# A two-layer trunk kernel: opening products and loads in written order, other modulations later, h written straight from x

## The chip, the cores and the metric

The kernel runs on one core of a Trainium2 chip. The metric is the device time of one execution in microseconds (us). Before the change it is 1355.4 us, the median of 3 runs (1355.3 to 1356.14).

## What is computed

Two transformer layers work on 128 prompt tokens and 256 sample tokens (384 rows of 2048 numbers, float32). Each layer first makes a modulation from two condition vectors (one for the prompt, one for the samples), then normalises and modulates its input, and projects it:

```
m = silu(cond) @ w_mod + b_mod            # w_mod is 2048 x 6144
shift, scale, gate = split(m, 3)
h = rmsnorm(x, g) * (1 + scale) + shift   # 384 x 2048
u = h @ w_in                              # layer 0: 2048 x 7680; layer 1: 2048 x 5120
x = x + gate * (mixer(u) @ w_out)
```

The mixer of layer 0 is a gated linear recurrence beside attention with grouped heads, that of layer 1 windowed attention. Nothing of layer 0 after h can start before shift and scale are known, and these need 33.5 MB of w_mod.

## The kernel before, in words

Products of the projections run on TensorE (PE) in float32r, in three products each: a number is split in a high part, rounded by ScalarE (ACT), and the remainder, made by VectorE (DVE). For the weights these are `whi` and `wlo`, for the activations `hh` and `hl`; the products are hi·hi, hi·lo and lo·hi.

The opening of layer 0 works in five phases over k, the 16 blocks of 128 rows of the weights: blocks 0; 1 and 2; 3 to 5; 6 to 9; 10 to 15 (`START`, line 38). In each phase `start_products` runs six groups of 512 columns of w_in. A group has four accumulators `mm` (128x384 each); for each of its weight pieces (one or two blocks, 256 or 512 KB) `w_piece` loads `raw`, ACT casts it to `whi`, DVE makes `wlo`, and PE runs 12 products for a block, 24 for two. At the end of a group ACT copies (first phase) or DVE adds (later ones) the four accumulators into an SBUF tile. So there are 6, 6, 12, 12 and 18 weight pieces and 72, 144, 216, 288 and 432 products in the five phases.

While a phase's products run, `start_mod` (line 740) makes the shift and scale columns of the next phase: it loads w_mod in pieces `mraw` of 512 KB (8 pieces for two blocks, 4 for one), multiplies each with the padded condition columns `cs32` on PE into one bank `px`, copies the bank to `ev` (ACT), turns it with 128x128 transposes (PE), sums four rows of it (`ms`, DVE), and adds bias and gain (`modc`, `acol`, DVE). `modulate` (line 460) then scales x (tile tE for blocks 0 to 3, tF, tG, tH for the others) by the row of 1/rms `rb0` (DVE), applies scale and shift (ACT, in place), casts the result to `hh` (ACT) and makes `hl` (DVE). Only then can the products of that block start.

A second stream of work, the units (`mods`, line 776), makes the modulation of layer 1 and the gates of layer 0 on DVE: each unit loads 512 KB of w_mod (also a tile named mraw, line 271, in a ring of three) and adds it into `acc` with two instructions. `pump` (line 348) decides after each weight piece whether units are issued: it adds a rate to a budget (0.6 per piece in the opening, `RATE0`), and also asks that a running estimate of DVE's time stay below that of PE. All must be done near the end of layer 0's output projection.

All these loads go through the one queue of SyncE (SP), which issues in order; a load waits there for its buffer. The opening's w_mod pieces have a ring of four buffers (`RAWB`), its weight pieces a ring of three (`SRAW`). A scheduler in the framework decides the order of the instructions on each engine from dependences, priorities and its own estimate of time; the program's text decides only where these tie.

## Time and profile before

| | |
|---|---|
| runs, median (lowest to highest) | 1355.4 us (1355.3 to 1356.14) |
| profiled execution: time / span | 1356.77 us / 1355.0 us |
| mean granted clock of TensorE | 0.993 of full |
| PE, DVE, ACT, POOL busy | 97%, 75%, 48%, 5% of the span |
| read from HBM | 256 MB |

Times of a trace are microseconds from the start of the span. Waits of an instruction are put down to what released it last. An engine's busy time counts an instruction from its start to its modelled end, and matmuls overlap, so the distance from one start to the next tells more than the length of one.

### The profile page before, as it was taken

The numbers are of one execution on the slowest core, as the hardware profiler recorded it, in microseconds if no ns is written. First come the engines' busy times: TensorE is split into PE (matmuls) and PEld (weight loads), VectorE is DVE, ScalarE is ACT, GpSimd is POOL, SyncE is SP. The second block draws the span as 40 slices with busy tenths as digits, with TensorE's granted clock in tenths as the row PEclk, the third lists the DMA queues.
The fourth block names the chain that finished last, engine by engine and source line by source line (L and its number), as shares of the span: only waits on it lengthen the run. The fifth ranks groups of instructions, "written<-read, shape, count | busy, mean of one in ns | idle before, by whom it ended". The sixth has DMA issues, their size and how long they took to land.

```text
span 1355.0 us, 19101 instructions
## 1 busy us (share of the span) xinstructions
PE 1321.0 (97%) x7093; PEld 1125.7 (83%) x7093; DVE 1019.0 (75%) x1602; ACT 647.9 (48%) x1297; POOL 72.4 (5%) x84
## 2 busy tenths in 40 slices
PE   5899999999999999999999999999999999999998
PEld 4678888997888878787987887888888999998887
DVE  5678757998998745896998969995656664499743
ACT  4532233476655534755433347345766763352221
POOL 1000000000000021101000000200000101000000
PEclk8899999999999999999999999999999999999999
DMA  9989989755555334576778854784332345457642
GB/s 284 304 289 331 317 289 319 236 160 179 176 174 181 97 106 138 167 232 201 242 244 254 297 184 133 234 283 119 92 94 81 104 118 166 129 181 254 210 152 84
DMA packets 138317, 265.42 MB, mean 196 GB/s; under 512 B 8944, under 2 KB 46768, under 8 KB 138224
## 3 DMA queue, kind: packets, MB, share of 16 engines
q1 hardware_dynamic: 132592, 246.52, 56.9%
q0 software_dynamic: 5376, 17.60, 4.5%
q8 instruction: 56, 0.92, 0.3%
q14 instruction: 37, 0.30, 0.1%
q10 hardware_dynamic: 256, 0.08, 0.0%
HBM read 256.04 MB, written 8.13 MB: 195 GB/s over the span
## 4 chain that ended last, share of the span: by engine, by line
PE 91%; DMA 4%; DVE 3%; ACT 1%; POOL 1%; issue 0%; DVEq 0%; ACTq 0%; SPq 0%; POOLq 0%
PE mm L77 77%; PE px L77 14%; DMA raw<-in_l_w_in_dram 2%; DMA mraw<-in_l_w_mod_dram 1%; DVE wlo L77 1%; DVE acc L77 1%; DMA tB<-in_x_sample_dram 0%; ACT whi L370 0%; POOL sm L444 0%; DVE tB L77 0%; DMA rowc<-in_c_dram 0%; DVE tG L77 0%; ACT tE L469 0%; DVE tH L77 0%; POOL r L444 0%
## 5 line engine op out<-in xcount | busy, mean ns | idle before, releaser
L370 ACT CAST whi<-raw 128x1024 fp32r<-128x1024 f32 (+1 forms) x270 | 278.4, 1032 | 500.1 <-PE mm L77 393.7
L77 DVE TENSOR_TENSOR wlo<-raw,whi 128x1024 fp32r<-128x1024 f32 (+1 forms) x270 | 323.4, 1198 | 188.0 <-PE mm L77 148.6
L77 PE MATMUL mm<-whi,hh 128*128 128x512 f32 x1008 | 398.9, 396 | 0.0
L77 PE MATMUL mm<-wlo,hh 128*128 128x512 f32 x1008 | 391.7, 391 | 3.2 <-DVE wlo L77 3.2
L77 PE MATMUL mm<-whi,hl 128*128 128x512 f32 x1008 | 393.5, 391 | 0.6 <-DVE hl L77 0.6
L77 DVE SCALAR_TENSOR_TENSOR acc<-mraw,csil,acc 128x1024 f32<-128x1024 f32 x240 | 299.0, 1279 | 9.0 <-DMA mraw<-in_l_w_mod_dram 9.0
L77 PE MATMUL mm<-hh,whi 128*128 128x384 f32 x768 | 264.4, 347 | 7.1 <-ACT hh L471 4.6
L77 PE MATMUL mm<-hl,whi 128*128 128x384 f32 x768 | 259.2, 338 | 0.0
L77 PE MATMUL mm<-hh,wlo 128*128 128x384 f32 x768 | 254.5, 338 | 0.2 <-DVE wlo L77 0.2
L77 PEld LDWEIGHTS mm<-wlo,hh 128*128 128x128 f32 x1008 | 189.3, 188 | 42.7 <-DVE wlo L77 5.8
L77 PEld LDWEIGHTS mm<-whi,hl 128*128 128x128 f32 x1008 | 189.3, 188 | 40.8 <-DVE hl L77 1.5
L77 PEld LDWEIGHTS mm<-whi,hh 128*128 128x128 f32 x1008 | 189.4, 188 | 39.3 <-ACT tE L824 0.8
L77 PEld LDWEIGHTS mm<-hh,whi 128*128 128x128 f32 x768 | 145.3, 190 | 22.2 <-issue 10.1
L77 PEld LDWEIGHTS mm<-hh,wlo 128*128 128x128 f32 x768 | 144.8, 189 | 2.7 <-DVE wlo L77 1.0
L77 PEld LDWEIGHTS mm<-hl,whi 128*128 128x128 f32 x768 | 145.5, 190 | 1.2 <-issue 0.2
L623 ACT ACTIVATE p<-px,nb,rs 128x384 f32<-128x384 f32 (+1 forms) x72 | 42.4, 596 | 15.0 <-DVE nb L77 14.5
L77 PE MATMUL px<-mraw,cs 128*32 128x256 f32 (+1 forms) x576 | 40.4, 377 | 4.9 <-DMA mraw<-in_l_w_mod_dram 4.9
L633 ACT ACTIVATE p<-p,sum 128x384 f32<-128x384 f32 (+1 forms) x72 | 36.1, 540 | 15.1 <-DVE sum L77 13.2
L77 DVE TENSOR_REDUCE mx<-px 128x1 f32<-128x384 f32 (+1 forms) x54 | 29.7, 567 | 9.3 <-PE px L77 8.9
L77 PEld LDWEIGHTS px<-mraw,cs 128*32 128x32 f32 x576 | 16.3, 114 | 20.0 <-issue 8.2
L77 PEld LDWEIGHTS px<-ct,p 128*128 128x128 f32 x168 | 20.1, 141 | 8.3 <-issue 2.8
L444 POOL TENSOR_TENSOR rs<-rs,nhalf 128x12 f32<-128x12 f32 x6 | 14.7, 2450 | 227.5 <-DVE rs L77 227.5
(415 smaller groups left out, 1228.5 us busy)
## 6 DMA issues: line engine op xcount, KB each, us to landing
raw<-in_l_w_in_dram SPq DMA_DIRECT2D x194, 512.0 KB, 3.9
mraw<-in_l_w_mod_dram SPq DMA_DIRECT2D x192, 512.0 KB, 5.0
raw<-in_l_w_out_dram SPq DMA_DIRECT2D x64, 512.0 KB, 4.9
raw<-in_l_w_in_dram SPq DMA_DIRECT2D x12, 256.0 KB, 6.6
tK<-in_l_b_mod_dram POOLq DMA_DIRECT2D x6, 256.0 KB, 6.0
y1d<-tA POOLq DMA_DIRECT2D x2, 768.0 KB, 5.2
tD<-y1d POOLq DMA_DIRECT2D x2, 768.0 KB, 6.0
tL<-y1d POOLq DMA_DIRECT2D x2, 768.0 KB, 6.2
```

The source lines that it names most:

```text
L77: return f(*a, **k)
L370: nc.scalar.copy(hi, raw)
L444: nc.gpsimd.tensor_tensor(out=out, in0=out, in1=nhalf[:, 0:out.shape[1]], op=ALU.pow)
L623: nc.scalar.activation(p[:, j], ss[j], AF.Exp, bias=nb[:, j:j + 1], scale=rs[:, i + j:i + j + 1], accum_out=sm[:, j:j + 1])
L633: nc.scalar.activation(p[:, j], p[:, j], AF.Copy, scale=sm[:, j:j + 1])
```

## The change

Six edits, all in the opening of layer 0.

- **Order.** In the first two phases the products, w_mod products and transposes on PE, and the loads of weights and of w_mod on SP, keep the order of the program's text (`pin`).
- **Units.** The rate is a list by phase: none in the first two, 0.6 in the third and fourth, 1.0 in the fifth. A unit's load is issued behind the last weight load of the text. By program order, 7 units' loads stood in the first two phases before and none now; VectorE's accumulations (two per unit) stand at 14, 32 and 61 after the second, fourth and fifth phase before, at 0, 28 and 56 now; they are level at 96 some 50 weight pieces after the opening, and from there PE's order is almost the same to the end.
- **Idle tiles.** Six of the eight w_mod pieces for blocks 1 and 2 go to the tiles of hh and hl of later blocks, which are idle then, and not to the ring of four.
- **h from x.** For the first block of a phase ACT writes `hh` straight from x with scale and shift, and DVE computes the modulated x in place for `hl`; the other blocks go through x as before. The work goes block by block.
- **Scaling by rb0.** Instead of within `modulate`, each block's product with `rb0` stands at the start of its modulation; those of later blocks are ordered behind the first `hl`.
- **Pace.** The next phase's modulation is spread over one weight piece less (two in the first phase), with a step of its own between the copy to `ev` and the transposes.

```
-RATE0 = 0.6
+RATE0 = (0.0, 0.0, 0.6, 0.6, 1.0)
...
+    last_w = [None]
+    pinned = {"t": False, "s": False}
+    def pin(ins, queue):
+        if pinned[queue]:
+            tc.keep_in_program_order(ins)
+        return ins
...
-            nc.sync.dma_start(raws[kt], I[f"l{l}_w_mod"][kt * P:kt * P + P, c0:c0 + 1024])
+            with tc.issue_after(last_w[0].ins):
+                nc.sync.dma_start(raws[kt], I[f"l{l}_w_mod"][kt * P:kt * P + P, c0:c0 + 1024])
...
-        nc.sync.dma_start(raw, w_view(w, kt, nk, c0, n))
+        last_w[0] = pin(nc.sync.dma_start(raw, w_view(w, kt, nk, c0, n)), "s")
...
-    def modulate(l, q, xt, rb, hq=None, parts=((0, 4),)):
-
-        hh, hl = hq_tiles(q) if hq is None else hq
-        for k0, k1 in parts:
-            x = xt[:, k0:k1]
-            nc.vector.tensor_tensor(out=x, in0=x, in1=rb.unsqueeze(1).broadcast_to([P, k1 - k0, T]), op=ALU.mult)
-            for k in range(k0, k1):
-                for c, s in CT:
-                    kt = 4 * q + k
-                    nc.scalar.activation(xt[:, k, s], xt[:, k, s], AF.Identity, bias=modc[l][:, kt, c:c + 1],
-                                         scale=acol[l][:, kt, c:c + 1])
-            nc.scalar.copy(hh[:, k0:k1], x)
-            nc.vector.tensor_tensor(out=hl[:, k0:k1], in0=x, in1=hh[:, k0:k1].bitcast(F32), op=ALU.subtract)
-        return hh, hl
+    def modulate(k, first):
+        x, (hh, hl) = xT[k // 4][:, k % 4], [t[:, k % 4] for t in h0[k // 4]]
+        for c, s in CT:
+            m, a = modc[0][:, k, c:c + 1], acol[0][:, k, c:c + 1]
+            nc.scalar.activation(hh[:, s] if first else x[:, s], x[:, s], AF.Identity, bias=m, scale=a)
+            if first:
+                nc.vector.tensor_scalar(out=x[:, s], in0=x[:, s], scalar1=a, scalar2=m, op0=ALU.mult, op1=ALU.add)
+        if not first:
+            nc.scalar.copy(hh, x)
+        return nc.vector.tensor_tensor(out=hl, in0=x, in1=hh.bitcast(F32), op=ALU.subtract)
...
-    h0 = [hq_tiles(q) for q in range(4)]
+    h0 = [hq_tiles(0)]
+    done0 = []
+    idle = ["hh1", "hl1", "hh2", "hl2", "hh3", "hl3"]
...
-                    nc.tensor.matmul(ps[c][:, 0:T], lhsT=wh, rhs=hh[:, kq], start=(kt + k == k0), stop=False)
...
+                    pin(nc.tensor.matmul(ps[c][:, 0:T], lhsT=wh, rhs=hh[:, kq], start=(kt + k == k0), stop=False), "t")
...
+            for i in range(k, k + nk):
+                x = xT[i // 4][:, i % 4]
+                if k:
+                    with tc.issue_after(done0[0].ins):
+                        nc.vector.tensor_tensor(out=x, in0=x, in1=rb0, op=ALU.mult)
+                else:
+                    nc.vector.tensor_tensor(out=x, in0=x, in1=rb0, op=ALU.mult)
...
-                    raw = wpool.tile([P, k8, n], F32, tag="raw", bufs=RAWB, name=nm("mraw"))
-                    nc.sync.dma_start(raw, w_view(I["l0_w_mod"], k8 * i, k8, D * (1 - part) + k * P, n))
+                    if k == 1 and idle:
+                        raw = hpool.tile([P, 4 * T], F32, tag=idle.pop(0), name=nm("mraw"))[:, 0:1024]
+                        raw = raw.rearrange("p (k c) -> p k c", k=k8)
+                    else:
+                        raw = wpool.tile([P, k8, n], F32, tag="raw", bufs=RAWB, name=nm("mraw"))
+                    pin(nc.sync.dma_start(raw, w_view(I["l0_w_mod"], k8 * i, k8, D * (1 - part) + k * P, n)), "s")
...
-                        nc.tensor.matmul(ps[32 * (j % 4):32 * (j % 4) + 32, part * n:part * n + n],
-                                         lhsT=cs32[:, kt, :], rhs=raw[:, j], start=(kt < 4), stop=(kt >= KT - 4))
+                        pin(nc.tensor.matmul(ps[32 * (j % 4):32 * (j % 4) + 32, part * n:part * n + n],
+                                             lhsT=cs32[:, kt, :], rhs=raw[:, j], start=(kt < 4), stop=(kt >= KT - 4)), "t")
...
             nc.scalar.copy(ev[:, 0:2 * n], ps[:, 0:2 * n])
+            yield
             cp = px()
             for b in range(2 * nk):
-                nc.tensor.transpose(cp[:, b * P:b * P + P], ev[:, b * P:b * P + P], ident)
+                pin(nc.tensor.transpose(cp[:, b * P:b * P + P], ev[:, b * P:b * P + P], ident), "t")
...
-            modulate(0, k // 4, xT[k // 4], rb0, h0[k // 4], ((k % 4, k % 4 + nk),))
+            for i in range(k, k + nk):
+                if len(h0) <= i // 4:
+                    h0.append(hq_tiles(i // 4))
+                m = modulate(i, i == k0)
+                done0.append(m)
             yield
...
-    pace[1] = RATE0
+    pinned["t"] = pinned["s"] = True
...
+        pace[1] = RATE0[i]
         nxt, n_nxt = iter(()), 0
         if i + 1 < len(phases):
             k2, k3 = phases[i + 1]
-            nxt, n_nxt = start_mod(k2, k3), 4 * (k3 - k2)
-        n = len(first) * len(pairs(k0, k1))
+            nxt, n_nxt = start_mod(k2, k3), 4 * (k3 - k2) + len(pairs(k2, k3))
+        n = len(first) * len(pairs(k0, k1)) - (2 if i == 0 else 1)
         done = 0
         for j, _ in enumerate(start_products(k0, k1)):
-            while done < (j + 1) * n_nxt // n:
+            while done < min(n_nxt, (j + 1) * n_nxt // n):
                 next(nxt, None)
                 done += 1
             pump()
         for _ in nxt:
             pass
+        pinned["t"] = pinned["s"] = i < 1
         if i == 1:
             load_params()
```

On SP, at the start of the first phase's weights, before the change (raw: weights; line 748: w_mod of the opening; line 271: units; the tiles' numbers tell them apart):

```order
L368 DMA raw_328<-in_l_w_in_dram 128x512
L748 DMA mraw_347<-in_l_w_mod_dram 128x4x256
L368 DMA raw_361<-in_l_w_in_dram 128x512
L748 DMA mraw_379<-in_l_w_mod_dram 128x4x256
L368 DMA raw_393<-in_l_w_in_dram 128x512
L748 DMA mraw_411<-in_l_w_mod_dram 128x4x256
L748 DMA mraw_417<-in_l_w_mod_dram 128x4x256
L271 DMA mraw_424<-in_l_w_mod_dram 128x1024
L271 DMA mraw_426<-in_l_w_mod_dram 128x1024
L368 DMA raw_436<-in_l_w_in_dram 128x512
L748 DMA mraw_454<-in_l_w_mod_dram 128x4x256
L271 DMA mraw_460<-in_l_w_mod_dram 128x1024
```

And now, in the same place (line 379: weights, line 771: w_mod of the opening):

```order
L379 DMA raw_323<-in_l_w_in_dram 128x512
L771 DMA mraw_344<-in_l_w_mod_dram 128x4x256
L771 DMA mraw_350<-in_l_w_mod_dram 128x4x256
L379 DMA raw_364<-in_l_w_in_dram 128x512
L771 DMA mraw_382<-in_l_w_mod_dram 128x4x256
L771 DMA mraw_388<-in_l_w_mod_dram 128x4x256
L379 DMA raw_402<-in_l_w_in_dram 128x512
L771 DMA mraw_420<-in_l_w_mod_dram 128x4x256
L771 DMA mraw_426<-in_l_w_mod_dram 128x4x256
L379 DMA raw_440<-in_l_w_in_dram 128x512
L771 DMA mraw_458<-in_l_w_mod_dram 128x4x256
L771 DMA mraw_464<-in_l_w_mod_dram 128x4x256
```

Two w_mod pieces now stand between one weight piece and the next, and the three loads of units are gone from here.

On PE, at the end of the first phase, before (mm: products, the number tells the accumulator; px<-mraw: w_mod products, px<-ct,ev: the transposes; mm_503 is of the phase's last group, mm_561 of the next phase's first):

```order
L77 MATMUL mm_503<-hh_42_254,wlo_508 128x384
L77 MATMUL px_346<-mraw_522,cs_109 32x256 x4
L77 MATMUL px_346<-mraw_528,cs_109 32x256 x4
L77 MATMUL px_536<-ct,ev_534 128x128 x4
L77 MATMUL px_595<-mraw_596,cs_109 32x128 x8
L77 MATMUL px_595<-mraw_606,cs_109 32x128 x8
L77 MATMUL mm_561<-hh_42_254,whi_567 128x384
L77 MATMUL mm_562<-hh_42_254,whi_567 128x384
```

And now (mm_439 is of the fourth group of six, mm_495 of the fifth):

```order
L77 MATMUL mm_439<-hh_42_254,wlo_444 128x384
L77 MATMUL px_341<-mraw_458,cs_109 32x256 x4
L77 MATMUL px_341<-mraw_464,cs_109 32x256 x4
L77 MATMUL px_472<-ct,ev_470 128x128 x4
L77 MATMUL mm_495<-hh_42_254,whi_501 128x384
L77 MATMUL mm_495<-hl_43_255,whi_501 128x384
L77 MATMUL mm_495<-hh_42_254,wlo_503 128x384
L77 MATMUL mm_496<-hh_42_254,whi_501 128x384
```

The transposes that lead to blocks 1 and 2 stood behind all 72 products of the first phase, with only w_mod products between them and the products that need blocks 1 and 2; now the 24 products of the last two groups stand between.

On DVE, from the first scaling by rb0 (tE to tH: x of blocks 0 to 3, 4 to 7, and so on), before:

```order
L77 TENSOR_TENSOR tE_133<-tE_133,rb_238 128x384
L77 TENSOR_TENSOR tE_133<-tE_133,rb_238 128x768
L77 TENSOR_TENSOR tE_133<-tE_133,rb_238 128x384
L77 TENSOR_TENSOR tF_160<-tF_160,rb_238 128x768 x2
L77 TENSOR_TENSOR tG_187<-tG_187,rb_238 128x768
L77 TENSOR_REDUCE ms_314<-px_311 128x4
L77 TENSOR_TENSOR wlo_332<-raw_328,whi_330 128x512
L77 TENSOR_TENSOR modc_122<-ms_314,par 128x2 x2
L77 TENSOR_TENSOR tG_187<-tG_187,rb_238 128x768
L77 SCALAR_TENSOR_TENSOR acol_124<-modc_122,par 128x2
L77 TENSOR_TENSOR tH_217<-tH_217,rb_238 128x768
```

And now:

```order
L77 TENSOR_TENSOR tE_133<-tE_133,rb_238 128x384
L77 TENSOR_REDUCE ms_309<-px_306 128x4
L77 TENSOR_TENSOR wlo_327<-raw_323,whi_325 128x512
L77 TENSOR_TENSOR modc_122<-ms_309,par 128x2 x2
L77 SCALAR_TENSOR_TENSOR acol_124<-modc_122,par 128x2
L77 TENSOR_SCALAR tE_133<-tE_133,acol_124,modc_122 128x128
L77 TENSOR_SCALAR tE_133<-tE_133,acol_124,modc_122 128x256
L77 TENSOR_TENSOR hl_43_255<-tE_133,hh_42_254 128x384
L77 TENSOR_TENSOR tE_133<-tE_133,rb_238 128x384 x3
```

The sum `ms` and what follows it for block 0 stood among the scalings of all 16 blocks; now they and the first `hl` come right after the scaling of block 0.

## Rows read from the trace of the kernel before

**Rows 1.** The page, part 1: busy time, share, instructions of each engine

```profile
PE 1321.0 (97%) x7093; PEld 1125.7 (83%) x7093; DVE 1019.0 (75%) x1602; ACT 647.9 (48%) x1297; POOL 72.4 (5%) x84
```

**Rows 2.** Windows, all engines: busy us (instructions), TensorE clock, DMA share, GB/s

```profile
58.00:92.00 34.00, 33.76 (x238) 29.94 (x242) 26.23 (x42) 8.52 (x11) 0.60 (x1) 0.92 0.85 287
...
92.00:214.00 122.00, 120.15 (x872) 97.88 (x861) 84.13 (x131) 38.38 (x56) 0.00 (x0) 1.00 0.93 311
...
214.00:290.00 76.00, 75.21 (x433) 75.20 (x434) 71.82 (x79) 42.51 (x51) 1.43 (x2) 1.00 0.71 233
...
440.00:500.00 60.00, 60.00 (x341) 50.93 (x340) 35.15 (x79) 29.53 (x71) 9.77 (x10) 1.00 0.36 103
```

**Rows 3.** Windows of 2 us around the starts of two stages

```profile
46.00:48.00 2.00, 2.00 (x14) 1.14 (x13) 1.28 (x1) 1.33 (x4) 0.00 (x0) 1.00 1.04 304
...
60.00:62.00 2.00, 2.00 (x8) 2.00 (x8) 0.85 (x3) 0.74 (x1) 0.00 (x0) 0.50 1.09 355
```

**Rows 4.** Windows: a full and an idle stretch of the DMA engines

```profile
26.00:48.00 22.00, 17.98 (x110) 12.92 (x103) 14.01 (x20) 12.75 (x28) 0.00 (x0) 0.84 1.04 355
...
66.00:70.00 4.00, 4.00 (x51) 3.69 (x49) 3.40 (x6) 0.00 (x0) 0.00 (x0) 1.00 0.03 8
```

**Rows 5.** Timeline of PE, first phase: start, length, instruction, wait before it

```profile
23.95 0.44 PE L77 MATMUL px<-ct,ev 128*128 128x128 f32 x2 [0.55 <-ACT ev L756]
...
29.41 1.08 PE L77 MATMUL px<-mraw,cs 128*32 128x256 f32 x8 [2.81 <-DMA mraw<-in_l_w_mod_dram]
...
30.43 1.01 PE L77 MATMUL mm<-hh,whi 128*128 128x384 f32 x2
```

**Rows 6.** Timeline of DVE, the chain to the first product

```profile
25.28 0.17 DVE L77 TENSOR_REDUCE ms<-px 128x4 f32<-128x16 f32 x1
...
25.37 0.68 DVE L77 TENSOR_TENSOR wlo<-raw,whi 128x512 fp32r<-128x512 f32 x1
...
25.96 0.23 DVE L77 TENSOR_TENSOR modc<-ms,par 128x2 f32<-128x2 f32 x2
...
26.98 0.15 DVE L77 SCALAR_TENSOR_TENSOR acol<-modc,par 128x2 f32<-128x2 f32 x1
...
29.38 0.55 DVE L77 TENSOR_TENSOR hl<-tE,hh 128x384 fp32r<-128x384 f32 x1
```

**Rows 7.** Timeline of ACT, the same chain

```profile
27.16 0.99 ACT L469 ACTIVATE tE<-tE,modc,acol 128x128 f32<-128x128 f32 x2
```

**Rows 8.** Timeline of PE from the first phase into the second

```profile
44.02 0.45 PE L77 MATMUL mm<-hh,whi 128*128 128x384 f32 x1 [1.13 <-ACT whi L370]
...
49.95 1.07 PE L77 MATMUL px<-mraw,cs 128*32 128x256 f32 x16
...
57.97 1.65 PE L77 MATMUL mm<-hh,whi 128*128 128x384 f32 x4 [4.58 <-ACT hh L471]
...
60.05 0.52 PE L77 MATMUL mm<-hh,whi 128*128 128x384 f32 x1
...
60.38 0.52 PE L77 MATMUL mm<-hl,whi 128*128 128x384 f32 x1
```

**Rows 9.** Timeline of PE at the end of the second phase

```profile
91.38 1.07 PE L77 MATMUL px<-mraw,cs 128*32 128x256 f32 x16
...
92.38 0.44 PE L77 MATMUL mm<-hh,whi 128*128 128x384 f32 x1
...
93.18 0.63 PE L77 MATMUL px<-ct,ev 128*128 128x128 f32 x4
```

**Rows 10.** DMA issues, 0 to 60 us: form, count, KB each, median us to landing

```profile
mraw<-in_l_w_mod_dram SPq DMA_DIRECT2D x24, 512.0 KB, 7.7
```

**Rows 11.** DVE by form: busy us, mean ns of one, idle before

```profile
L77 DVE SCALAR_TENSOR_TENSOR acc<-mraw,csil,acc 128x1024 f32<-128x1024 f32 x240 | 299.0, 1279 | 9.0 <-DMA mraw<-in_l_w_mod_dram 9.0
```

**Rows 12.** Timeline of PE into the fifth phase

```profile
213.16 0.66 PE L77 MATMUL px<-ct,ev 128*128 128x128 f32 x4 [0.71 <-ACT ev L756]
...
214.79 0.44 PE L77 MATMUL mm<-hh,whi 128*128 128x384 f32 x1 [0.98 <-ACT whi L370]
```

More of the change, by code (lines that the diff above doesn't have):

```diff
@@ L729, in start_group @@
                     wh, wl = hi[:, k, c * P:c * P + P], lo[:, k, c * P:c * P + P]
[L730 to L732 removed]
+                    pin(nc.tensor.matmul(ps[c][:, 0:T], lhsT=wh, rhs=hh[:, kq], start=(kt + k == k0), stop=False), "t")
+                    pin(nc.tensor.matmul(ps[c][:, 0:T], lhsT=wh, rhs=hl[:, kq], start=False, stop=False), "t")
+                    pin(nc.tensor.matmul(ps[c][:, 0:T], lhsT=wl, rhs=hh[:, kq], start=False, stop=(kt + k == k1 - 1)), "t")
             yield
```

2 lines of the change are left out of this document (removed).

## The prediction

> **What bounds the kernel now.** I read the page's busy times first: PE is busy for 1321.0 of 1355.0 us [rows 1], so at most 34 us of open waiting can be won, and all work that PE does stays. Then the windows by stage. In the fifth phase (214 to 290) PE ends 433 products in 75.21 us, 0.174 us each [rows 2], without a wait: that is its pace at the full clock, and nothing in the opening is to be won there. The third and fourth phase (92 to 214) have 2 us of idle PE, at a DMA rate of 311 GB/s [rows 2] where a full stretch reaches 355 [rows 4]: bound by PE, with loads close behind. So what is left lies before 92 us. There the timelines show two holes. The first product starts at 30.43, although block 0's transposes ran at 23.95; between them PE took w_mod products of the next phase that waited 2.81 us for their load [rows 5], and DVE put its sums behind scalings of other blocks [rows 6]. From the first phase to the second PE waits 4.58 us for hh before 57.97 [rows 8], and then the granted clock stands at 0.50 [rows 3], the 1.2 GHz level: from 60.05 to 60.38 a product takes 0.33 us, not 0.174 [rows 8]. Last, the DMA engines idle from 66 to 70 us at 8 GB/s [rows 4], where by the program's order SP stands before a w_mod piece whose buffer, one of four, isn't free: the loads in front of 92 us are held by order and buffers, not by the DMA engines.
>
> **The first product.** The transposes at 23.95 stand in both kernels. Behind them DVE now has, with nothing between, the sum 0.17, one wlo 0.68, two modc 0.23 and acol 0.15 [rows 6]: 1.2 us, to 25.7 with small gaps. ACT then writes hh itself, two instructions in 0.99 us [rows 7], to 26.7; the cast behind them is gone. The second product needs hl: the in-place x on DVE, which no trace shows (between the 0.15 of a tiny instruction and the 0.55 of a subtraction over 384 columns [rows 6]; I take 0.3, since it is done in two parts), and hl's own 0.55 [rows 6]. Products flow from 27.6, 2.8 us earlier.
>
> **The first phase.** 72 products at 0.174 are 12.5 us. The first twelve fall behind a wait and are reckoned at 0.33: 1.8 more. Eight w_mod pieces go in four pairs; a pair takes 1.0 us from 91.38 to 92.38 [rows 9], and I add 0.25 for the turn to and from products: 5.0. The transposes now stand right behind the pair that they wait for, so PE waits for the copy ev (0.71) and runs them (0.6) [rows 12]: 1.3. ACT casts the fourth group's weights only behind the copies of the results before; for PE's wait I take another 0.7, as for ev. Together 21.3, to 48.9. The loads don't hold this: 14 pieces of the new order hold 5.2 MB up to the last w_mod piece, 14.8 us at 355 GB/s [rows 4], so 38 even if they start only at 23; PE asks for it at 43. Three loads of units that stood between them are gone, which matters little here for that reason.
>
> **Into the second phase.** The 24 products behind the transposes take 4.2 us and cover the chain to hh of block 1: DVE's sums without an accumulation of 1.28 [rows 11] among them, ACT's two instructions, hl. I leave 0.1: full pace at 49.0. Before, the stage starts at 57.97 and runs at half clock until about 62 [rows 3, 8], which is worth 2 us: full pace from 60.0. Gain here 11.0. If that cover is gone, the 4.58 us of [rows 8] come back, and the clock with them.
>
> **The second phase.** 144 products 25.1 us; six pairs of w_mod pieces 7.5; two copies with transposes, now in line, 2.6. Loads: SP keeps the text's order, so a weight piece waits behind w_mod pieces whose buffers are freed by products two steps back. A piece lands 7.7 us after its issue (median, [rows 10]), a step of PE takes 24 x 0.174 + 1.25 = 5.4. With one step of lead each of five steps would wait 2.3, 11.5 in all; with two it waits nothing. Four w_mod and three weight buffers give mostly two: I take 1.0. The end is 49.0 + 36.2 = 85.2. Before, the same work (20 w_mod pieces, their transposes, 144 products) is done at 93.18 + 0.6 less the four products that went ahead [rows 9], 93.1. The gain has shrunk to 7.9, mostly because the transposes now stop PE.
>
> **Third and fourth phase.** The next phase's h is ready one piece sooner, and the copy ev has a step to itself, so the waits of 0.71 and 0.98 at the start of the fifth phase [rows 12] go, and what is late next is nothing that the trace shows: 1.5 gained. Against it, units: 28 accumulations here instead of 18, so five loads more, 2.6 MB, 7.4 us at 355 GB/s if nothing were spare. Spare are 355 - 311 GB/s over 122 us, 5.4 MB [rows 2, 4]. The cost is between nothing and 7.4; I take 1.5, near the lower end, since the spare is twice the need, but not nothing, since part of it stands where SP waits for buffers. VectorE's ten accumulations of 1.28 [rows 11] find 38 us of idle time [rows 2], and so do the smaller scalings and the in-place x, a few us in all.
>
> **Behind the opening.** Five accumulations are owed after the fifth phase, up to 13 later, and all are paid 50 pieces after the opening: 16.6 us of VectorE, against 24.9 idle from 440 to 500 [rows 2], so at no cost; bounds -1 and +4 (a quarter of it in PE's way).
>
> **Sum.** -7.9 - 1.5 + 1.5 + 0 = -7.9 from 1356.8, the profiled execution (its span of 1355.0 and 1.8 around it): 1348.9. That execution is 1.4 over the median of the runs, so **1347.5** as a median. All at the good ends (no load waits, transposes hidden, no cost of units): some 15 less, 1340.5. Debt of loads in full and the gain at the fifth phase lost: 1354.5.
>
> **Rivals.**
> *The loads' debt.* The third and fourth phase turn load-bound, and what was won in front is given back there: up to 7.4. For it: the DMA share is 0.93 already [rows 2]. Against it: the spare above. 1353, from 1350.5 to 1355.
> *The queue in text order (slower).* In the second phase SP stands before a w_mod piece whose buffer isn't free while the weights behind it are wanted, as at 66 to 70 before [rows 4], now at every step. If no lead builds up, a step takes the landing, 7.7 [rows 10], and a wlo of 1.3 (twice the 0.68 of half the columns, [rows 6]), 9.0 against 5.4: 3.6 lost on each of five steps, 18 in place of the 1.0 above, so 9 slower than before: 1364.5; with half of that price no change. It decides from 1.8 us per step on, where the gain is gone. For it: one queue, in order, with waits for buffers. Against it: six idle tiles let the ring of four start the second phase empty.
> *The clock stays low.* The first phase now alternates products with waits. At half clock its 60 other products cost 0.15 more, 9 us, and nothing is left: 1355.5. Against it: a wait of 1.13 us before 44.02 [rows 8] left the clock at 1.00 [rows 3]; only after the 4.58 was it 0.50. I see no wait over 1.3 there.
> The Trainium skill, page "TensorE: Matmul & The Clock Gate", section "HAM oscillation — how this bites in real kernels", describes this: a wait for a load in each step lets the gate close, and every step starts cold. By that rule it would be this rival; the trace agrees with the rule for the long wait and shows no such thing for the short ones.
> *More.* The second phase has no load waits and the scheduler hides more: 1341.
>
> **How the numbers follow.** A run can tell 0.2% here, 2.7 us: faster is under 1352.7, slower over 1358.1. The forecast (gain 4 to 11) has 0.56, more 0.09, the debt 0.17, the clock 0.08, the queue 0.10. Faster: 0.56 + 0.09 + half of the debt 0.09 = 0.74. Slower: three quarters of the queue and a quarter of the clock, 0.10. The same: the rest, 0.16. The range 1340.5 to 1354.5 holds the forecast, most of more and of the debt and a little of the clock, 0.8. The forecast's own range is 1344 to 1351.5.
>
> **What would show it.** In the trace after: the first product near 27, the second behind hl at 27.6; the second phase's first product near 48.5 with the clock at 1.00 behind it, not 57.97 at 0.50; its last near 85; the fifth phase starting 8 us earlier than 214.79 without a wait for a cast before it; the rest of PE alike. I am wrong if PE waits for raw or whi at each step of 49 to 85 (queue), if PE's idle time and the DMA share of the third and fourth phase both rise (debt), if the clock is 0.50 through 30 to 45 (clock), or if PE waits for wlo between 300 and 540 (VectorE's debt).

## The result: 1.6% slower, and the profile after

The changed kernel takes 1378.8 us (median of 4 runs, 1374.8 to 1381.5) where the kernel before, run beside it, takes 1355.8: a ratio of 1.0164, 95% interval 1.0137 to 1.0192. The forecast was 1347.5. The profiled execution has 1379.4 us and a span of 1377.6, 22.6 more than before.

PE's work has not grown by much: first its line of the page (busy us, share of the span, instructions), then windows of the trace after (columns as in [rows 2]). They hold the first phase, the second, the third with the first half of the fourth, the second half of the fourth, and the fifth.

```profile
PE 1328.6 (96%) x7093; PEld 1130.3 (82%) x7093; DVE 1021.2 (74%) x1626; ACT 650.6 (47%) x1303; POOL 77.3 (6%) x84
```
```profile
24.00:52.00 28.00, 22.82 (x143) 17.02 (x144) 16.09 (x37) 18.02 (x38) 0.00 (x0) 0.86 0.89 274
52.00:91.00 39.00, 35.34 (x284) 30.41 (x283) 22.56 (x44) 11.84 (x18) 0.60 (x1) 0.97 0.77 260
91.00:177.00 86.00, 83.80 (x602) 68.12 (x600) 66.39 (x106) 23.71 (x36) 0.00 (x0) 1.00 0.91 306
177.00:226.00 49.00, 39.60 (x251) 32.32 (x252) 28.35 (x41) 15.67 (x23) 0.00 (x0) 0.93 0.85 294
226.00:300.00 74.00, 74.00 (x431) 72.87 (x430) 67.66 (x75) 33.94 (x38) 1.44 (x2) 1.00 0.66 212
```

The second half of the fourth phase stands out, not the first two phases: 9.4 of 49 us without work on PE, and part of the rest at half clock. The mean DMA share of 0.85 hides two things: the DMA engines ran dry (0.01) while SP stood, and were full again (0.99) while PE waited.

```profile
198.00:200.00 2.00, 2.00 (x27) 0.99 (x25) 0.96 (x1) 0.00 (x0) 0.00 (x0) 1.00 0.01 2
...
216.00:218.00 2.00, 0.00 (x0) 0.00 (x0) 0.56 (x1) 2.00 (x4) 0.00 (x0) 1.00 0.99 345
```

The sharpest view is one that counts. Every trace holds the same 5328 products of the projections in the same sequence of phases (72, 216, 432, 720 and 1152 at the phases' ends), so the start of the n-th one can be compared between kernels. In the table below "before" gives its start in us, each other row the difference to it; `r` is the ratio to the runs of before, with its interval. The differences belong to the profiled execution, whose time stands beside the median.

| kernel | median | r | profiled | 1 | 72 | 96 | 216 | 432 | 576 | 672 | 720 | 864 | 1352 | 5328 |
|---|---|---|---|---|---|---|---|---|---|---|---|---|---|---|
| before | 1355.8 | | 1356.8 | 30.4 | 49.7 | 64.7 | 91.1 | 142.1 | 177.2 | 200.0 | 211.1 | 239.7 | 336.9 | 1349.9 |
| after | 1378.8 | 1.0164 [1.0137, 1.0192] | 1379.4 | −3.9 | +1.9 | −7.7 | −1.3 | −1.2 | −1.5 | +4.1 | +12.9 | +10.9 | +19.4 | +22.6 |
| e1 | 1372.1 | 1.0116 [1.0091, 1.0141] | 1369.2 | −3.5 | +1.8 | −9.1 | −3.3 | −3.7 | −2.3 | −2.6 | −2.0 | +2.1 | +9.2 | +12.5 |
| e2 | 1371.5 | 1.0109 [1.0085, 1.0133] | 1380.4 | −4.6 | +1.3 | −8.4 | +0.6 | +2.6 | +1.9 | +8.3 | +18.4 | +16.5 | +16.6 | +23.5 |
| e3 | 1366.3 | 1.0079 [1.0053, 1.0105] | 1365.0 | −3.4 | +1.0 | −9.8 | −3.5 | −5.2 | −8.3 | −6.3 | −4.0 | +0.4 | +8.2 | +7.6 |
| e4 | 1376.8 | 1.0148 [1.0124, 1.0173] | 1378.6 | −4.1 | −0.6 | −9.7 | −8.8 | −7.2 | −8.2 | −2.6 | +11.6 | +9.7 | +17.3 | +21.3 |
| e5 | 1364.6 | 1.0064 [1.0045, 1.0083] | 1363.8 | −0.9 | −3.9 | −4.3 | −6.1 | −5.1 | −5.4 | −6.2 | −5.0 | −0.3 | +7.4 | +6.9 |
| e6 | 1366.7 | 1.0079 [1.0058, 1.0099] | 1370.0 | −4.0 | −0.5 | −9.5 | −8.3 | −9.8 | −11.2 | −5.7 | +8.1 | +6.2 | +13.7 | +13.3 |
| e7 | 1359.3 | 1.0019 [1.0008, 1.0030] | 1358.0 | −4.4 | −2.3 | −11.3 | −8.8 | −10.4 | −11.2 | −7.1 | +3.0 | +1.0 | +1.2 | +1.2 |
| e8 | 1367.9 | 1.0083 [1.0065, 1.0100] | 1365.9 | −3.8 | +1.0 | −9.9 | −6.4 | −7.3 | −9.8 | −6.2 | +3.8 | +1.9 | +9.1 | +8.9 |
| e9 | 1353.5 | 0.9974 [0.9960, 0.9988] | 1355.3 | −4.0 | −0.4 | −9.4 | −7.7 | −7.8 | −6.4 | −6.8 | −6.2 | −1.5 | −1.7 | −1.8 |
| e10 | 1358.2 | 1.0012 [0.9996, 1.0028] | 1356.7 | −4.9 | +0.1 | −10.8 | −4.3 | −6.9 | −6.9 | −7.7 | −7.4 | −0.1 | −0.3 | −0.4 |
| e11 | 1354.0 | 0.9981 [0.9968, 0.9994] | 1357.3 | −2.1 | +2.0 | −7.1 | −6.1 | −6.9 | −5.4 | −5.8 | −5.2 | +0.1 | −0.2 | +0.4 |
| e12 | 1355.0 | 0.9976 [0.9960, 0.9992] | 1352.7 | −3.3 | +3.6 | −5.4 | −2.7 | −5.3 | −4.0 | −3.9 | −3.4 | −5.0 | −5.3 | −4.2 |
| e13 | 1370.7 | 1.0101 [1.0084, 1.0119] | 1367.7 | −4.2 | +0.4 | −10.5 | −5.6 | −5.8 | −7.5 | −5.0 | +3.2 | +1.2 | +8.3 | +10.9 |
| e14 | 1358.9 | 1.0015 [1.0002, 1.0029] | 1358.4 | −4.5 | +0.4 | −8.7 | −7.5 | −8.8 | −10.0 | −6.2 | +4.1 | +2.1 | +1.9 | +1.6 |
| e15 | 1355.7 | 0.9992 [0.9982, 1.0002] | 1355.3 | −5.0 | −0.6 | −9.7 | −7.9 | −8.4 | −10.3 | −9.2 | −0.8 | −2.1 | −2.3 | −1.7 |
| e16 | 1352.9 | 0.9973 [0.9964, 0.9983] | 1351.6 | −4.4 | −2.3 | −11.4 | −10.5 | −12.6 | −13.0 | −12.1 | −11.5 | −5.2 | −5.4 | −5.4 |
| e17 | 1346.5 | 0.9930 [0.9916, 0.9943] | 1348.5 | −4.4 | +0.3 | −8.7 | −7.7 | −9.3 | −9.7 | −8.9 | −8.3 | −8.2 | −8.4 | −8.4 |
| e18 | 1363.8 | 1.0058 [1.0046, 1.0071] | 1363.8 | −4.0 | −0.5 | −9.5 | −5.2 | −6.4 | −6.6 | −4.4 | −4.8 | −5.1 | −7.0 | +6.9 |

The row "after" splits the 22.6 us: −1.5 up to the 576th product (of 7.7 won at the 96th), +5.6 to the 672nd, +6.8 over the seam into the fifth phase to the 864th, +8.5 to the 1352nd, +3.2 behind.

How firm is a column? By the program's order PE, ScalarE, VectorE and SP do the same work in the same order in e6, e7 and e14 up to the 1300th product, in the changed kernel and e2 likewise, and in e16 and e17 up to about the 720th. Their rows still differ by up to 2.8 us at the 216th product and 5.5 at the 720th. So a difference of that size between two single traces can be the execution alone; the medians are firmer.

**The first two phases.** The hole of 4.58 us before 57.97 [rows 8] is gone: the second phase's first product, the 73rd, starts at 51.94 without a wait. PE's waits from the first product to the end of the second phase, and that product (start, length, instruction, the wait in brackets):

```profile
26.57 0.45 PE L77 MATMUL mm<-hh,whi 128*128 128x384 f32 x1 [2.16 <-ACT hh L476]
27.61 0.69 PE L77 MATMUL mm<-hl,whi 128*128 128x384 f32 x1 [0.60 <-DVE hl L77]
44.66 0.66 PE L77 MATMUL px<-ct,ev 128*128 128x128 f32 x4 [0.71 <-ACT ev L779]
49.48 0.44 PE L77 MATMUL mm<-hh,whi 128*128 128x384 f32 x1 [1.53 <-ACT tK L747]
51.94 0.53 PE L77 MATMUL mm<-hh,whi 128*128 128x384 f32 x1
64.23 0.44 PE L77 MATMUL px<-ct,ev 128*128 128x128 f32 x2 [0.49 <-ACT ev L779]
71.52 0.44 PE L77 MATMUL mm<-hh,wlo 128*128 128x384 f32 x1 [0.64 <-DVE wlo L77]
78.24 0.44 PE L77 MATMUL mm<-hh,whi 128*128 128x384 f32 x1 [1.18 <-ACT whi L381]
79.50 0.44 PE L77 MATMUL mm<-hh,wlo 128*128 128x384 f32 x1 [0.64 <-DVE wlo L77]
85.29 0.66 PE L77 MATMUL px<-ct,ev 128*128 128x128 f32 x4 [0.71 <-ACT ev L779]
```

The first product comes at 26.57 as forecast. At 49.48 the last group of the first phase (its 64th product) waits for an accumulator that ScalarE's copies of the group before (tK) have not emptied yet. In ScalarE's order they stand behind the modulation of blocks 1 and 2:

```profile
47.20 0.98 ACT L476 ACTIVATE hh<-tE,modc,acol 128x128 fp32r<-128x128 f32 x2
...
48.96 0.46 ACT L747 COPY tK<-mm 128x384 f32<-128x384 f32 x1
```

SP meanwhile stands before buffers (its queue; a long entry is a wait inside the row). Of the two windows below, the first shows the half clock in which the second phase starts, the second that the DMA engines then run dry:

```profile
47.41 2.81 SPq L379 DMA_DIRECT2D raw<-in_l_w_in_dram  x1
...
57.97 5.76 SPq L771 DMA_DIRECT2D mraw<-in_l_w_mod_dram  x3
...
64.39 6.11 SPq L771 DMA_DIRECT2D mraw<-in_l_w_mod_dram  x3
```
```profile
52.00:54.00 2.00, 2.00 (x8) 2.00 (x7) 0.00 (x0) 1.42 (x2) 0.00 (x0) 0.50 0.99 315
54.00:60.00 6.00, 6.00 (x61) 5.55 (x60) 4.75 (x7) 1.06 (x1) 0.00 (x0) 0.98 0.12 33
```

**The fourth phase.** SP first, then PE. SP stands from 193.87 to 199.6 inside a pair of w_mod pieces; the weight piece behind them is issued only at 200.16, and PE waits for its cast at 207.15, then 3.92 us before 218.23, still in the fourth phase; the starts that follow are 0.32 us apart for a while, not 0.174. By the program's order three weight loads for the work behind the opening stand in SP's queue ahead of the weight that 218.23 waits for. It is issued at 209.86, lands at 216.4 in full DMA engines, and its cast on ScalarE (217.15, last fence) comes 0.8 later, behind the scalings of the next phase's blocks.

```profile
193.87 5.70 SPq L771 DMA_DIRECT2D mraw<-in_l_w_mod_dram  x2
199.62 0.50 SPq L282 DMA_DIRECT2D mraw<-in_l_w_mod_dram  x1
200.16 0.42 SPq L379 DMA_DIRECT2D raw<-in_l_w_in_dram  x1
...
209.86 0.47 SPq L379 DMA_DIRECT2D raw<-in_l_w_in_dram  x1
```
```profile
179.01 0.45 PE L77 MATMUL mm<-hh,whi 128*128 128x384 f32 x1 [2.04 <-ACT whi L381]
...
207.15 0.44 PE L77 MATMUL mm<-hh,whi 128*128 128x384 f32 x1 [1.78 <-ACT whi L381]
...
213.66 0.66 PE L77 MATMUL px<-ct,ev 128*128 128x128 f32 x4 [0.71 <-ACT ev L779]
218.23 0.69 PE L77 MATMUL mm<-hh,whi 128*128 128x384 f32 x1 [3.92 <-ACT whi L381]
```
```profile
214.97 1.37 ACT L476 ACTIVATE tH<-tH,modc,acol 128x128 f32<-128x128 f32 x3 [1.37 <-DVE acol L77]
...
217.15 1.03 ACT L381 CAST whi<-raw 128x1024 fp32r<-128x1024 f32 x1
```

**At 336 us.** A unit's modulation ends here (its sums at 333.49, its copy ev on ScalarE, its transposes). ScalarE is behind, because Exp (L895, L896) and Ln (L856, L857) of the next heads alternate and each turn loads a table. Behind the wait the clock is at 0.50 (the window below): the twelve products after the transposes start 0.43 us apart, before the wait 0.23, which is some 2.4 us more, so the wait of 5.74 makes most of the 8.5.

```profile
333.49 1.06 PE L77 MATMUL px<-acc,ct 128*32 128x512 f32 x8
335.75 0.40 PE L77 MATMUL mm<-whi,hl 128*128 128x512 f32 x1
341.89 0.90 PE L77 MATMUL px<-ct,ev 128*128 128x128 f32 x3 [5.74 <-ACT ev L311]
```
```profile
344.00:346.00 2.00, 2.00 (x6) 1.53 (x5) 1.15 (x1) 0.68 (x2) 0.00 (x0) 0.50 0.50 104
```
```profile
322.32 1.04 ACT L381 CAST whi<-raw 128x1024 fp32r<-128x1024 f32 x1
323.37 1.28 ACT L856 ACT_TABLE_LOAD   x1
324.67 0.71 ACT L856 ACTIVATE tE<-tB,ct,lb 128x384 f32<-128x384 f32 x1
325.39 1.28 ACT L895 ACT_TABLE_LOAD   x1
...
327.23 1.28 ACT L857 ACT_TABLE_LOAD   x1
...
329.16 1.28 ACT L896 ACT_TABLE_LOAD   x1
...
333.31 1.28 ACT L856 ACT_TABLE_LOAD   x1
...
341.25 0.58 ACT L311 COPY ev<-px 128x512 f32<-128x512 f32 x1
```

The whole run has 11 table loads, before 7.

**Behind.** VectorE's waits for the units' loads (us in all, times, the longest) after, before, and in e3:

```profile
DVE acc L77 <- DMA mraw<-in_l_w_mod_dram: 34.8, 19, 5.3
```
```profile
DVE acc L77 <- DMA mraw<-in_l_w_mod_dram: 9.0, 7, 4.1
```
```profile
DVE acc L77 <- DMA mraw<-in_l_w_mod_dram: 7.1, 4, 3.6
```

### The profile page after: what moved, and what is told of

Read it like the earlier page. It is cut to its first block, busy times and chain, and to the rows that moved or that the text cites. A ratio compares the mean times of both kernels' runs of the same rounds, so it can differ in the third digit from the quotient of the medians.

```text
span 1377.6 us, 19123 instructions
## 1 busy us (share of the span) xinstructions
PE 1328.6 (96%) x7093; PEld 1130.3 (82%) x7093; DVE 1021.2 (74%) x1626; ACT 650.6 (47%) x1303; POOL 77.3 (6%) x84
## 4 chain that ended last, share of the span: by engine, by line
PE 84%; DVE 5%; DMA 5%; ACT 3%; issue 1%; POOL 1%; SPq 0%; ACTq 0%; DVEq 0%; POOLq 0%
PE mm L77 71%; PE px L77 14%; DMA raw<-in_l_w_in_dram 2%; DVE acc L77 2%; DMA mraw<-in_l_w_mod_dram 1%; DVE wlo L77 1%; ACT whi L381 1%; DVE tB L77 0%; DMA tC<-in_x_sample_dram 0%; POOL rs L455 0%; DMA rowa<-in_l_norm_dram 0%; DMA tab<-in_l_b_knorm_dram 0%; DVE tG L77 0%; DVE tH L77 0%; ACT junk L567 0%
## 5 line engine op out<-in xcount | busy, mean ns | idle before, releaser
L77 PE MATMUL mm<-hh,whi 128*128 128x384 f32 x768 | 266.8, 347 | 14.2 <-ACT whi L381 10.5
L77 PEld LDWEIGHTS mm<-hh,whi 128*128 128x128 f32 x768 | 146.0, 190 | 28.8 <-ACT whi L381 14.8
L641 ACT ACTIVATE p<-p,sum 128x384 f32<-128x384 f32 (+1 forms) x72 | 35.4, 540 | 13.2 <-DVE sum L77 11.3
L455 POOL TENSOR_TENSOR rs<-rs,nhalf 128x12 f32<-128x12 f32 x6 | 21.7, 3612 | 221.3 <-DVE rs L77 221.3
```

Of the source, the lines that this page charges most:

```text
L77: return f(*a, **k)
L455: nc.gpsimd.tensor_tensor(out=out, in0=out, in1=nhalf[:, 0:out.shape[1]], op=ALU.pow)
L641: nc.scalar.activation(p[:, j], p[:, j], AF.Copy, scale=sm[:, j:j + 1])
```

## The experiments

The theory after the first look: separate costs, one for each place above, and the dealing alone behind the fourth phase. The rivals were two of the forecast's: the debt of the units' loads, and the queue in text order.

**e1, the old dealing.** Where `n_nxt` turns of the next phase's modulation are dealt over `n` weight pieces of a phase; in the fourth phase the changed kernel deals 27 turns over 11 pieces, here it is 24 over 12 as before:

```
-nxt, n_nxt = start_mod(k2, k3), 4 * (k3 - k2) + len(pairs(k2, k3))
+gap = i < 2    # start_mod yields behind ev only with gap
+nxt, n_nxt = start_mod(k2, k3, gap), 4 * (k3 - k2) + (len(pairs(k2, k3)) if gap else 0)
...
-n = len(first) * len(pairs(k0, k1)) - (2 if i == 0 else 1)
+n = len(first) * len(pairs(k0, k1)) - (2 if i == 0 else 1 if i == 1 else 0)
```

> The changed kernel, but from the third phase on the w_mod pieces are dealt out as before: two per group of products in the fourth phase (24 pieces over 12 groups, no extra turn behind the copy ev), not 27 turns over 11. Theory (pacing): the 14 us that the changed kernel loses between the 432nd and the 720th product (PE waits 8.0 us for whi there, because three w_mod pieces in a row stand before a weight piece) go; the 720th product comes near 212 instead of 224, and the time is near 1366 (1363 to 1370) against 1378.8. Rival (debt of the units' loads): the 28 units' loads are still there and the fourth phase still loses over 8 us; 1374 or more.

The 720th product is 2.0 ahead: 1.7 lost since the 432nd where 14.1 were. The time gained only 6.7 and misses: 4.1 of the 14 only moved behind the 720th, and ScalarE's order changed along with it, to 13 table loads; to the 1352nd 7.1 were lost in another way (PE waits 4.3 for wlo at 310 to 345).

**e2, ev on VectorE.** `nc.scalar.copy(ev, ps)` in mod_part becomes `nc.vector.tensor_copy(ev, ps)`.

> The changed kernel, but the copy ev of a later modulation (mod_part) is made by VectorE instead of ScalarE. Theory (ScalarE's order): PE's wait of 5.74 us before 341.89 and the clock at half speed behind it come from ScalarE, whose Exp and Ln now alternate with a table load of 1.28 us each time; with the copy on VectorE, which is idle at 335 to 337, the 1352nd product stands about 11 later than before instead of 19.4, and the time is near 1370.5 (1368 to 1374). Rival (the sums themselves are late, or VectorE is as late as ScalarE): the wait stays over 3 us and the time over 1375.

From the 864th to the 1352nd 0.1 are lost instead of 8.5, and the median falls by 7.2, to the theory's time. (The profiled execution is 9 above the median; its 720th product is 5.5 later than in the changed kernel with the same order of work up to there.) ScalarE's loads fell to 9 as well, so the copy's new place and the order are not told apart; that the wait was ScalarE's is shown.

**e3, units' loads free.** `with tc.issue_after(last_w[0].ins):` taken away in mod_acc.

> The changed kernel, but the loads of the later modulations may be moved ahead of weight loads again, as before (no issue_after). Theory (late loads): VectorE's waits for mraw fall from 34.8 us towards the 9.0 of before, and the 4.6 us that the changed kernel loses behind 940 us go; the opening is touched by less than that: near 1374 (1371 to 1377). Rival (the loads go into the first two phases instead, ahead of their weights): the second phase gets longer by 4 us or more, and the time is 1379 or over.

Waits for mraw fall to 7.1, and nothing is lost behind the 1352nd any more, as expected; but the time misses: the gain is 12.5, since from the 432nd to the 720th only 1.2 are lost too. The theory had no reason for that. The edit also moved other loads: by the program's order SP's queue differs from the changed kernel's from the second phase on.

**e4, no text order.** `pinned` stays False.

> The changed kernel, but products and loads of the first two phases are not kept in the text's order. Theory (text order wins in the first phase and gives it back in the second): the 96th product stands at 60 or later instead of 57.0, the 216th within 3 us of 89.8, and the time is within 4 us of 1378.8. Rival (the queue in text order, which the prediction named as the slower case, is the cause): the 216th product comes before 86 and the time is under 1372.

The theory's time, but not its opening: without the order the 96th product is 9.7 ahead and the 216th still 8.8. So the order gives nothing in front and costs 7.5 by the 216th product, in the direction of the forecast's rival; the fourth phase then lost 18.8 and hid it.

**e5, the units' shift alone**, on the kernel before: `RATE0 = (0.0, 0.0, 0.6, 0.6, 1.0)`, `pace[1] = RATE0[i]` in the loop.

> The kernel before with one thing of the change: the later modulations get no turn in the first two phases (the list of rates 0, 0, 0.6, 0.6, 1.0); their loads may still be moved ahead of weights. Theory (the shift of these units by itself changes ScalarE's order): ScalarE gets 13 table loads where it had 7, and PE loses 4 to 9 us between the 1152nd and the 1352nd product as in the changed kernel; the opening is at most 3 us shorter: near 1360 (1356 to 1365) against 1356. Rival (the shift costs nothing, and relieves the first two phases of nine loads of 0.5 MB): 1352 or less.

The opening gains 6.1 at the 216th, more than thought; 4.8 go between the 432nd and the 864th, 7.7 from there to the 1352nd. ScalarE has 13 table loads. Moving the units is enough to bring a cost of that size in this stretch, though PE's waits fall otherwise: 3.75 for wlo before 322.28, where VectorE had stood 5.23 for ScalarE's Exp, and 2.24 for ev before 332.59.

**e6 to e8, combinations**: e6 is e3 and e4 together, e7 adds e2, e8 is e3 with only PE's products pinned, not the loads.

> The changed kernel without both orders: products and loads of the first two phases not kept in the text's order, and the units' loads free to go ahead of weights. Theory (the two costs add): the opening as without text order (the 216th product near 8.8 ahead of before, against 3.5 ahead with free loads alone), the fourth phase as with free loads (0 to 1 lost), the loss of 7.8 at the 1352nd product stays: near 1360 (1356 to 1363). Rival (free units' loads take the place of weights in the unpinned opening): the 216th product within 4 us of before and the time 1364 or more.

> As the run before (neither order), with the copy ev of a later modulation on VectorE. Theory (three separate causes): the wait of 5.8 for ev at the 1352nd product goes too, and about 8 us with it: near 1351 (1348 to 1355), faster than before. Rival (the ev's place in ScalarE's order stands for a delay that returns elsewhere): 1356 or more.

> The changed kernel with the units' loads free, and of the first two phases only PE's products kept in the text's order, not SP's loads. It tells which of the two orders costs the 6.3 us between the 96th and the 216th product. Theory (the queue of loads in text order, which stands before w_mod pieces whose buffers are not free): the loss falls to 2 us or less, 216th product 7 or more ahead of before, near 1362 against 1366. Rival (PE in text order, where transposes and products wait in line for ev, hh and wlo): the loss stays over 4 us and the time within 2 of 1366.

e6 misses: the opening adds up (−9.8 at the 432nd), but the fourth phase loses 17.9 with free loads, so e3's good one was not due to free loads alone. In e7 the cost at 336 us is gone (0.2 for 7.5), and the time misses by as much as the fourth phase. e8 divides the cost of the order at the 216th product: 3.5 ahead with both queues pinned, 6.4 with PE alone, 8.3 with none: 2.9 of SP, 1.9 of PE. Executions of the same order differ by up to 2.8 there, so the division is not shown; and its time, 1367.9, is no better than e3's and e6's.

**e9 to e12, all three undone**: e9 has e1, e2, e3 and e4, and in hgrn_prep holds each Ln behind the last Exp written before it (`with tc.issue_after(lexp[0].ins):`). e10 puts the text order back, e11 takes the idle tiles away (`idle = []`), e12 gives the units 0.6 in all phases.

> The changed kernel without either order (text order of the first two phases, units' loads behind weights), with two w_mod pieces per group from the third phase on as before, the ev of later modulations on VectorE, and the Ln of the next heads' preparation held behind the last Exp written before it, so that ScalarE changes tables less often. Left of the change: h straight from x, weights in idle tiles of h, units from the third phase on. Theory (the costs add): 11 us ahead at the 576th product as in the run before, still 8 to 10 ahead at the 720th, 4 lost at the seam to the fifth phase, nothing at the 1352nd: near 1350.5 (1347 to 1354). Rival (what is won in the opening meets the next bound, the loads of the fourth phase, whatever the pacing): 1355 or more.

> As the run before, but with products and loads of the first two phases in the text's order, as in the changed kernel. It prices that order with the other costs gone. Theory (the order costs at the second phase's steps what it costs with free loads): the 216th product 3.5 ahead of before where it is 8.8 without, and 5 to 7 us more than the run before: near 1356.5 (1353 to 1360). Rival (the order costs nothing, since what it loses in the second phase comes back in the third and fourth): within 2 us of the run before.

> As the first of these four runs, but the second phase's w_mod pieces go into the ring of four and not into idle tiles of h. Theory (the idle tiles let loads of the second phase start early): the 96th product comes 2 to 4 us later and the time is 1352.5 to 1354.5. Rival (without text order SP brings those loads early enough into the ring): within 1.5 us of the first run.

> As the first of these four runs, but the later modulations take their turns from the first phase on, at 0.6 per piece as before. Theory (the units' loads of the first two phases cost the opening what their removal gained alone, 4 to 6 us at the 216th product): 216th product 3 to 5 ahead of before, the fourth phase 1 to 2 shorter, near 1354 (1351 to 1357). Rival (the shift wins nothing in the end, since the loads come back in the third and fourth phase): 1351 or less.

e9 is faster than before, 0.9974, and its time is in the theory's range, but it is 6.4 ahead at the 576th product, not 11, and 4.7 went between the 720th and the 864th. The order's price is 4.7 us (e10 to e9, medians), a little under the theory; for the idle tiles the medians show nothing clear of noise (0.4; 2.3 at the 96th product, gone by the end: the rival). e12 is 5 less ahead at the 216th than e9, and in time not to be told from it; it is 3.4 ahead of e9 at the 864th: it loses nothing at that seam.

**e13 to e16, the dealing**: e13 is the changed kernel with a fifth w_mod buffer from the third phase on; e14 is e9 with the new dealing, e15 with only the `- 1`, e16 with only the turn behind ev.

```
+elif turn[0] % 5 == 4:
+    raw = spool.tile([P, k8, n], F32, tag="xw", bufs=1, name=nm("mraw"))
...
+turn[0] += k > 2
```

> The changed kernel with a fifth buffer for w_mod pieces from the third phase on (one more tile takes every fifth piece). Theory (SP stands before a w_mod piece whose buffer, one of four, is not free, while the weight piece behind it is wanted): the 14.1 us lost between the 432nd and the 720th product fall to 6 or less, and the time to 1366 to 1372. Rival (the fourth phase is short of load bandwidth, or of ScalarE): the loss stays at 11 or more and the time at 1375 or more.

> The version with all three undone, with the changed kernel's dealing of w_mod pieces in the third and fourth phase put back (a turn of its own behind ev, and all turns one group sooner: 27 over 11). Theory (this dealing is what costs the fourth phase): 10 to 15 us lost between the 432nd and the 720th product where that version lost 1.6, and a time of 1361 to 1368 against 1353.6. Rival (it needs the units' loads bound behind the weights, or another order besides): loss under 4, time under 1357.

> As the version with all three undone, but the w_mod pieces are dealt out one group sooner, without a turn of their own for ev (24 turns over 11 groups in the fourth phase). Theory (three w_mod pieces in a row are what hurts, and 24 over 11 has that in two groups, 27 over 11 in five): about 2/5 of the loss of the full dealing, 4 to 7 us between the 432nd and the 720th product. Rival (the last group without w_mod pieces is no loss at all): under 3.

> As the version with all three undone, but the copy ev of the opening's modulations has a turn of its own (27 turns over 12 groups in the fourth phase). Theory (three in a row in three groups of twelve, one of the three turns often empty): 2 to 5 us lost between the 432nd and the 720th product. Rival (it is the turn of ev that moves the pieces against the ring of four): 8 or more.

From the 432nd to the 720th product e14 loses 12.9, as its theory says, e15 7.6 and e13 9.0, both over theirs, e16 1.1, under it; e14's time is under its theory, e13's within. The columns between show why: two things were taken for one.

*The dealing.* From the 432nd to the 672nd product the six traces with the changed kernel's dealing and one order of SP's queue (after, e2, e4, e6, e7, e14) lose 2.7 to 5.8. All nine with turns over 12 pieces (e1, e5, e9 to e12, e16 to e18) lie between 1.1 gained and 2.0 lost, e13 with its fifth buffer loses 0.8, and e15 gains 0.8. By the program's order the dealing puts three w_mod pieces in a row four times: two of them are behind PE before the 576th product, where nothing is lost yet, and the loss comes behind it (after 5.6, e14 3.8 from the 576th). A row of three does not decide alone: in e3 and e8 the same dealing stands in another order of the queue, with such rows too, and they gain 1.1 and lose 1.1. In the medians the dealing costs 5.4 (e14 to e9), and the turn behind ev alone nothing (e16 to e9).

*The seam.* From the 672nd to the 864th, over the seam into the fifth phase, nearly all lose, whatever the dealing: after 6.8, e14 8.3, e15 7.1, e16 6.9, e13 6.3, e9 5.3, e1 4.7, e3 6.7, e5 5.9, the rest up to there 5.9 to 12.3; only e12 loses nothing. The dealing sets on which side of the 720th that falls.

**e17 and e18, the seam into the fifth phase.** In SP's order two to four weight loads for the work behind the opening stand ahead of the fifth phase's first weight, with the new dealing ahead of the fourth phase's last one too; in before there are two, in e12 none. e17 is e16 with an edge against that (w5 is the third weight load of the fifth phase); e18 adds rates of 0, 0.6, 0.6, 0.6, 0.6.

```
+with tc.issue_after(w5[0].ins) if tag == "raw" else nullcontext():
     last_w[0] = pin(nc.sync.dma_start(raw, w_view(w, kt, nk, c0, n)), "s")
```

> The best version so far (a turn for ev, the rest as all three undone), but the first weights of the work behind the opening may not be loaded ahead of the fifth phase's first three weight pieces. Theory (at the seam into the fifth phase the wanted weight stands behind two to four loads for later: PE waits 3.1 us for whi, then runs at half clock): 11.5 us ahead at the 720th product, still 10 or more ahead at the 864th instead of 5.2; near 1348 (1345.5 to 1351) against 1352.9. Rival (the later loads, now later themselves, are missed at the end of the fifth phase, or the loss at the seam is the units' debt of loads): 5 to 7 ahead at the 1352nd product, 1351.5 to 1355.

> As the run before, with the units' turns from the second phase on at 0.6 each, so that none are owed. Theory (the units' loads in the second phase cost PE there, and are nothing gained later once the seam is in order): 2 to 4 us less ahead at the 432nd product, near 1351 (1348 to 1354). Rival (what the shift wins in the opening is debt in the fourth and fifth phase in any case): within 1 us of the run before or faster.

e17 takes 1346.5 us, 0.9930 of before: the fastest of all, and the theory's time. From the 672nd to the 864th it loses 0.7, e16 6.9. At the 720th it is 8.3 ahead, not 11.5, though its order of work up to there is e16's: that part is the execution. At the seam in e16 (SP, ScalarE, PE) two later weights and a unit's load go first; the wanted weight is issued at 197.73 and lands 6.5 us later, its cast can start only at 204.29 (the view puts that wait down to DVE, but the load is what came last), and PE waits for that. Behind it two windows of e17: the last part of the fourth phase up to the seam, with the DMA engines full, and the fifth phase.

```profile
191.06 0.37 SPq L379 DMA_DIRECT2D raw<-in_l_w_in_dram  x1
195.62 0.37 SPq L379 DMA_DIRECT2D raw<-in_l_w_in_dram  x1
196.04 1.63 SPq L282 DMA_DIRECT2D mraw<-in_l_w_mod_dram  x1
197.73 0.43 SPq L379 DMA_DIRECT2D raw<-in_l_w_in_dram  x1
```
```profile
204.29 1.04 ACT L381 CAST whi<-raw 128x1024 fp32r<-128x1024 f32 x1 [2.68 <-DVE acc L77]
```
```profile
205.39 0.69 PE L77 MATMUL mm<-hh,whi 128*128 128x384 f32 x1 [3.07 <-ACT whi L381]
```
```profile
169.00:203.00 34.00, 33.45 (x228) 26.96 (x226) 23.43 (x31) 9.59 (x13) 0.00 (x0) 1.00 1.01 346
203.00:282.00 79.00, 79.00 (x467) 76.60 (x467) 73.60 (x87) 37.47 (x43) 1.44 (x2) 1.00 0.70 231
```

e18 was badly dealt: its rates sum to 28.8 units by the end of the opening, not 32.4 as in before and e17, so units were owed after all. They fall due near 716 us, and PE waits for VectorE's last sums, through ScalarE's cast:

```profile
716.09 0.79 PE L77 MATMUL px<-ahi,ones_r 128*128 128x512 f32 x1 [9.62 <-ACT ahi L337]
```

Its time misses. Up to the 1352nd product e18 is 7.0 ahead, so its question is half answered: nothing is lost at the seam, with more of the units moved or with fewer.

## Why the prediction was wrong, step by step

- **First product near 27, the next at 27.6.** Right: 26.57 and 27.61.
- **First phase, 21.3 us.** Too short by some 3: the 72nd product is 1.9 later than before. The wait of 1.53 for the copies tK (49.48) was in no term, the products behind it run at half clock, 0.32 apart, and so does the first pair of w_mod pieces, 1.9 us at 31.43 and not 1.0.
- **Into the second phase, full pace at 49.0.** Wrong. The chain to hh is covered, as said, and the 73rd product waits for nothing; but it starts at 51.94, and the clock is 0.50 at 52 to 54, which was to have gone. The cover had a price that was not counted: with hh moved forward in ScalarE's order the copies of the first phase's results stand behind it.
- **Second phase, load waits 1.0.** Undersized: PE waits 2.5 for weights there (71.52, 78.24, 79.50). The text order costs 3.4 (e10 to e9) to 7.5 us (after to e4) by the 216th product, so the slower rival "queue in text order" had the direction, at less than its price; how much of it is SP's, and how much PE standing in line for ev and tK, is open. By the forecast's own count the work done at 93.1 before is done at 90.0, 3 us sooner and not 7.9.
- **Third and fourth phase, −1.5 + 1.5 = 0.** This step failed most: 12.1 us from the 432nd product to the 864th. The extra turn was counted as a gain (the wait for ev; 0.71 of it is still there at 213.66) and the pace as nothing. What the forecast left out is the order in SP's queue. 27 turns over 11 weight pieces put three w_mod pieces in a row before SP's ring of four where two were; SP falls behind, and the weights come late: 2.7 to 5.8 lost by the 672nd product with this order of the queue, at most 2.0 with the turns over 12 pieces, 0.8 with a fifth buffer. And the loads for later work go ahead of the wanted weights at the seam: 6.8 here, 5 to 12 in the others with such loads ahead, 0.7 with the order mended (e17). The rival "debt" named the right stage, but not the cause: with the five more units' loads still there e17 loses 1.1 in all of it. Bandwidth is still part of the price: the DMA engines are full at the seam (1.01 in e17's window at 346 GB/s), so each load of 512 KB put ahead takes some 1.5 us from the wanted one, an estimate from that window.
- **Behind the opening, 0 (−1 to +4).** The 3.2 behind the 1352nd product are inside the bounds, by another way: not VectorE's debt, but units' loads that `issue_after` binds behind weights through the whole kernel. In the kernels without that edge nothing is lost there (−0.6 to +1.1), e18's late units apart. The 8.5 around 336 us were in no term: with the units moved, ScalarE's order changes tables where one of them ends.
- **Range and rivals.** 1378.8 lies beyond all of them, since each took one mechanism alone and the costs came together. The rival of the clock did not come as stated (1.00 from 34 to 50 us), but the argument against it, no wait over 1.3, did not hold: behind waits of 1.53 (before 49.48) and 2.04 (before 179.01) the granted clock stood at 0.50 at 52 to 54 and 0.53 at 182 to 184. Two slips in the working change little: the clock rival's 9 us lead to 1356.5, not 1355.5, and the 5.2 MB are 12 pieces, not 14.

e4 and e6 lose 12 at the seam, the others 5 to 8. For e6 that is the execution, since e7 and e14 have its order of work and lose 8; for e4 it stays open. Before, with two later loads ahead as well, PE waits only 0.98 there [rows 12], because the wanted weight has more lead: it is issued at 207.24, 3.9 us before the 720th product (211.11), in e16 1.9 before it (197.73 to 199.62), and both land 6.4 to 6.5 us after their issue. That kernel, which came later to the seam, did not show what stood in its queue.
